# The down-projection's weight combinations of a hybrid decoder layer: summed by DMA in DRAM beside the input projection, instead of by VectorE during the up projection

## The chip, the cores and the metric

The kernel runs on one core of one Trainium2 chip. The metric is the device time of one execution in microseconds (us): the median of three runs before the change is 1322.26 us (1322.09 to 1323.52).

## The reference, cut to what matters

One layer of a decoder: an input projection into seven column groups, differential attention and a gated linear recurrence (HGRN2) on its parts, an output projection, and a feed-forward block with a short convolution. Sizes: 1024 tokens and 16 meta tokens, width 1024, feed-forward width 2816, all float32.

```python
a = rmsnorm(h, ln_mix_pre)
dq, dk, dv, hq, hf, hi, hg = split(a @ w_in)             # 28 column tiles of 128
mix = concat(diff_attention(dq, dk, dv), hgrn2(hq, hf, hi, hg)) @ w_out
h = h + rmsnorm(mix, ln_mix_post)
u = causal_conv3(rmsnorm(h, ln_ffn_pre) @ w_up) + conv_b # 2 x 2816 columns
gate, up = split(u)
y = (gelu(gate) * up) @ w_down                           # w_down is 2816 x 1024
h = h + rmsnorm(y, ln_ffn_post)
```

The change concerns `w_down`, cut into four quarters W11, W12, W21, W22 (1408 x 512 each).

## The kernel before, in words

**Precision.** Every float32 operand of a large product is split into a high part (a copy rounded to a shorter format, made by ScalarE) and a low part (raw minus high, made by GpSimd or VectorE: `split`, line 147). Three matmuls per pair of tiles (high x high, high x low, low x high) give the product.

**Stages, in order of time.** (1) Norm and transposes of the input, and the first three weight tiles. (2) The input projection: `dense` (line 726) takes 25 weight tiles, one after the other; each is loaded by two DMAs from SyncE (`load_m`, `load_split`, line 152), one tile ahead of its use, and split by ScalarE and GpSimd. A tile (hf, hq, hi, hg, dq, dk or dv of a head) is 3 groups of 24 matmuls. `interleave` (line 60) mixes these matmuls with attention (`attn`) or the recurrence (`hgrn_head`) of a head, whose products along a tree (`halve`, line 387: tiles `tt` and `t`) GpSimd makes too. (3) The output projection. (4) The up projection: 22 iterations `ft` (loop at line 1436; 0 and a part of 1 stand ahead of it), each with two token halves `p`. Products use a seven-multiplication scheme for 2 x 2 blocks (Strassen-Winograd), so sums of weight quarters and of partial results are formed: `unit` (line 1305) evacuates three banks, pa, pb and pc, through VectorE and ScalarE; the convolution's multiply-adds (tile `c`) are on VectorE too. (5) The down projection with the same scheme: 7 products x 11 steps.

**The part that changes.** Of the seven products of stage 5, four (numbers 5, 6, 7 and 4) need a combination of the quarters of `w_down`. These are formed ahead, during stage 4, by `down_sums` (line 1371): for each of 11 row blocks, four 128 x 512 tiles `wd` are loaded by SyncE, VectorE forms four differences, and SyncE stores each into a DRAM scratch `tsc`. One step of this generator is taken at four places of each iteration from `ft` 6 on (`SUMS`, line 35, and line 1442), so that its 55 steps last through `ft` 19. In stage 5 `w_in` (line 1396) loads the combinations back from `tsc` (tile `wi`).

**What orders the work.** TensorE's order is written out by hand. On the other engines a scheduler places instructions; `tc.issue_after(x)` holds an instruction back until `x` has been placed. Each engine takes its queue in order: an instruction that waits for a semaphore holds back all behind it. A DMA that SyncE or GpSimd issues can itself wait for an earlier DMA.

Of the kernel before, what the change touches and what calls it, by code (L numbers as in the profile page):

```python
# [9 lines left out]
F32 = mybir.dt.float32  # L10
# [3 lines left out]
ALU = mybir.AluOpType  # L14
# [17 lines left out]
WN = [258, 256]  # L32
C0 = [0, 514]
FA, FH, FO = 840, 800, 740
SUMS = 6


def start(i):
# [48 lines left out]
def layer_kernel(ctx: ExitStack, tc: tile.TileContext, x, meta, table, lbl, gpre, gpost, win,  # L87
# [59 lines left out]
    def split(hi, lo, raw, eng=None, after=None):  # L147
        A.copy(hi, raw)
        with nullcontext() if after is None else tc.issue_after(after.ins):
            (eng or G).tensor_tensor(lo, raw, hi.bitcast(F32), op=ALU.subtract)  # L150

    def load_split(src, name, where=None, bufs=4):
        raw = wp.tile([P, 512], F32, tag="wr", name=f"wr_{name}", bufs=3)
# [29 lines left out]
    last_load = []  # L183

    at_p_cm, ap_ = pool("attn", 1, "right")
    z_cm, zp = pool("pre", 2, "right")

    def load_m(m, name, where=None, bufs=4):
        return [load_split(win[m][:, 512 * c: 512 * (c + 1)], f"{name}_{c}", where, bufs) for c in range(2)]
# [533 lines left out]
                yield from values(i + 1)  # L723
        carry.append(pend.pop("tail"))

    def dense(tiles, preload=None):
        parts = preload
        for idx, (m, name, evac) in enumerate(tiles):
            if parts is None:
                parts = load_m(m, name)  # L730
            nxt = load_m(tiles[idx + 1][0], tiles[idx + 1][1]) if idx + 1 < len(tiles) else None
            for g in range(3):
                for step, c in enumerate(proj_group(g, parts, name, evac)):
                    if step == (8 if idx or g else 14):
                        flush()
                    yield c
            parts = nxt
# [190 lines left out]

    for h in range(HEADS):
        t_h, tiles_h = hgrn_in(h)  # L930
        interleave(dense(tiles_h), [attn(h, t_a)] + carried(), FA, 1500)
        if h < HEADS - 1:
            t_a, tiles_a = attn_in(h + 1)
            interleave(dense(tiles_a), [hgrn_head(t_h)] + carried(), FH, 1500)

    close(at_cm)
    wo_cm, wop = pool("wo", 7)
# [430 lines left out]
    for j in range(4, 7):  # L1368
        prep(7 + j)

    def down_sums():
        for k in range(NF // 2):
            b = {}
            for nm, kk, half in (("11", k, 0), ("12", k, 1), ("22", k + NF // 2, 1), ("21", k + NF // 2, 0)):
                b[nm] = dn.tile([P, 512], F32, tag="gk", name=f"wd{nm}_{k}")
                SY.dma_start(b[nm], wdown[P * kk: P * (kk + 1), 512 * half: 512 * (half + 1)])
            yield
            for j, d, p_, q_ in ((0, "11", "12", "11"), (2, "12", "22", "12"), (1, "22", "22", "11"), (3, "21", "21", "22")):
                V.tensor_tensor(b[d], b[p_], b[q_], op=ALU.subtract)
                SY.dma_start(tsc[j][P * k: P * (k + 1)], b[d])  # L1380
                yield

    NH = NF // 2
    LOOK = 3
    ORDER = (1, 2, 5, 6, 3, 7, 4)
# [19 lines left out]
    def operands(pr, k, loaded=None):  # L1405
        ga, gb, gc, gs = (keep[nm][:, k] if keep else None for nm in ("ga", "gb", "gc", "gs"))
        if pr == 1:
            a = loaded[0] if loaded else g_in(k, 0, "1")
        elif pr == 2:
            SY.dma_start(gb, g_src(k + NH, 0))  # L1410
            a = gb
        elif pr == 5:
            a = gs
        elif pr == 6:
            V.tensor_tensor(gs, gs, ga, op=ALU.subtract)
            a = gs
        elif pr == 3:
            V.tensor_tensor(gb, gb, gs, op=ALU.subtract)
            a = gb
        elif pr == 7:  # L1420
            V.tensor_tensor(ga, ga, gc, op=ALU.subtract)
# [12 lines left out]

    wd_sums = down_sums()
# [31 lines left out]
    def sums5(k):  # L1467
        SY.dma_start(keep["gc"][:, k], g_src(k, 1))
        b = g_in(k + NH, 1, "5")
        V.tensor_tensor(keep["gs"][:, k], keep["gc"][:, k], b, op=ALU.add)  # L1470
        SY.dma_start(keep["ga"][:, k], g_src(k, 0))

    steps = [(pr, k) for pr in ORDER for k in range(NH)]
# [36 lines left out]
    def evac(pr, m, py):  # L1510
        if pr == 1:
            A.copy(x1[:, m], py)
        elif pr == 2:
            V.tensor_tensor(c11[:, m], py, x1[:, m], op=ALU.add)
            squares(c11[:, m], m, 0)
            as_bias(m, 0)
            G.tensor_tensor(c11[:, m], c11[:, m], gfo[:, :512], op=ALU.mult)
        elif pr == 5:
            A.copy(x5[:, m], py)
        elif pr == 6:  # L1520
            V.tensor_tensor(u2[:, m], py, x1[:, m], op=ALU.add)
        elif pr == 3:
            c = u2[:, m]
            V.tensor_tensor(c, py, c, op=ALU.add)
            squares(c, m, 1)
            s_ = rstd(m, 1)
            hh = fp.tile([P, D], F32, tag="hh", name=f"hh{m}", bufs=2)
            SY.dma_start(hh, hsc[P * m: P * (m + 1), :])
            V.scalar_tensor_tensor(hh[:, :512], c11[:, m], s_, hh[:, :512], ALU.mult, ALU.add)
            G.tensor_tensor(c, c, gfo[:, 512:], op=ALU.mult)  # L1530
            V.scalar_tensor_tensor(hh[:, 512:], c, s_, hh[:, 512:], ALU.mult, ALU.add)
            SY.dma_start(out[P * m: P * (m + 1), :], hh)
        elif pr == 7:
            V.tensor_tensor(x1[:, m], py, x1[:, m], op=ALU.add)
            c = x5[:, m]
            V.tensor_tensor(c, c, x1[:, m], op=ALU.add)
            squares(c, 4 + m, 1)
            as_bias(4 + m, 1)
            G.tensor_tensor(c, c, gfo[:, 512:], op=ALU.mult)
        else:  # L1540
            c = x1[:, m]
            V.tensor_tensor(c, py, c, op=ALU.add)
# [99 lines left out]
```

## Time and profile before

| | |
|---|---|
| runs | 1322.26 us median |
| profiled execution | 1325.6 us, of which the span from first to last instruction is 1323.8 us |
| granted TensorE clock | 0.997 |
| busy: PE / DVE / ACT / POOL | 97% / 70% / 52% / 34% of the span |
| DMA | 165.00 MB, 123 GB/s of HBM traffic over the span |

PE is TensorE's matmuls, DVE is VectorE, ACT is ScalarE, POOL is GpSimd and SP is SyncE, which issues every DMA of the kernel before. In a row of a group or of a wait, `a<-b` means that tile a is written from tile b; L54 is the line of a helper that records every VectorE, ScalarE and GpSimd operation, so these are told apart by their tiles. "x11" counts instructions. A span time such as 820.69 counts from the first instruction.

### The profile page before, as it was taken

To read this page: it belongs to the slowest core of one execution; us is meant where nothing else is said; L and a number is where in the kernel's file an instruction comes from. 1 tells how busy PE (TensorE), PEld (TensorE's weight loads), DVE (VectorE), ACT (ScalarE), POOL (GpSimd) and SP (SyncE) were. 2 spreads that over 40 slices of the span, in tenths; PEclk is the share of its full clock that TensorE was granted. 3 is DMA by queue.
4 is the path that set the end of the run, shared out by engine and by line. 5 is a ranking of instruction groups with operands and counts; after the bars stand their busy time and mean duration, and the time that the engine had idled before them with its cause. 6 is when DMAs were issued, how large, how long until landed. Compare 5 with 4: busy or idle time off the path is not lost.

```text
span 1323.8 us, 26191 instructions
## 1 busy us (share of the span) xinstructions
PE 1286.8 (97%) x10172; PEld 1185.5 (90%) x10172; DVE 930.1 (70%) x1531; ACT 692.5 (52%) x1635; POOL 455.4 (34%) x340
## 2 busy tenths in 40 slices
PE   8999999999999999899999999999999999999997
PEld 7899999899999988677999999999999997888875
DVE  6464646465645564547997788989989967697586
ACT  8475466547544754246754444444444435454553
POOL 5211211121112111243077667676676730010121
PEclk9999999999999999999999999999999999999999
DMA  5111121112111335487232234545445428865363
GB/s 209 61 40 33 54 57 41 49 46 65 44 42 41 88 101 169 153 277 254 81 112 80 80 95 154 177 144 173 154 144 166 144 84 275 312 205 166 88 206 120
DMA packets 99427, 165.00 MB, mean 125 GB/s; under 512 B 10035, under 2 KB 34899, under 8 KB 99302
## 3 DMA queue, kind: packets, MB, share of 16 engines
q1 hardware_dynamic: 99302, 163.32, 37.8%
q8 instruction: 80, 1.31, 0.4%
q14 instruction: 45, 0.37, 0.1%
HBM read 122.65 MB, written 40.63 MB: 123 GB/s over the span
## 4 chain that ended last, share of the span: by engine, by line
PE 45%; DVE 11%; ACT 3%; issue 3%; DMA 2%; POOL 0%; SPq 0%; DVEq 0%; ACTq 0%; POOLq 0%
PE pd L1491 5%; PE pd L1492 5%; PE pd L1490 5%; DVE c L54 5%; PE pb L1316 4%; PE pb L1317 3%; PE pb L1318 3%; PE pa L1316 2%; PE pa L1317 2%; PE pa L1318 2%; PE pc L1316 2%; PE pc L1317 2%; PE pc L1318 2%; PE py L976 1%; PE py L972 1%
## 5 line engine op out<-in xcount | busy, mean ns | idle before, releaser
L1316 PE MATMUL pb<-t,uh 128*128 128x258 f32 x504 | 144.0, 286 | 8.9 <-DVE u L54 8.9
L1318 PE MATMUL pb<-t,ul 128*128 128x258 f32 x504 | 141.6, 281 | 0.0
L1317 PE MATMUL pb<-t,uh 128*128 128x258 f32 x504 | 141.6, 281 | 0.0
L1491 PE MATMUL pd<-wl,gh 128*128 128x512 f32 x308 | 122.0, 396 | 1.2 <-DVE wl L54 1.1
L1492 PE MATMUL pd<-wh,gl 128*128 128x512 f32 x308 | 121.7, 395 | 0.0
L1490 PE MATMUL pd<-wh,gh 128*128 128x512 f32 x308 | 121.7, 395 | 0.0
L54 POOL TENSOR_TENSOR c<-c,c 128x514 f32<-128x514 f32 (+1 forms) x44 | 75.2, 1709 | 121.1 <-ACT c L54 111.4
L1316 PEld LDWEIGHTS pb<-t,uh 128*128 128x128 f32 x504 | 95.4, 189 | 12.2 <-DVE u L54 12.1
L54 DVE SCALAR_TENSOR_TENSOR c<-uu,cwt,c 128x514 f32<-128x514 f32 (+1 forms) x88 | 89.2, 1023 | 19.3 <-ACT c L54 19.0
L1317 PEld LDWEIGHTS pb<-t,uh 128*128 128x128 f32 x504 | 95.6, 190 | 0.0
L1318 PEld LDWEIGHTS pb<-t,ul 128*128 128x128 f32 x504 | 95.2, 189 | 0.0
L1316 PE MATMUL pa<-t,uh 128*128 128x258 f32 (+1 forms) x336 | 95.2, 283 | 0.0
L1318 PE MATMUL pa<-t,ul 128*128 128x258 f32 (+1 forms) x336 | 95.0, 283 | 0.0
L1317 PE MATMUL pa<-t,uh 128*128 128x258 f32 (+1 forms) x336 | 94.8, 282 | 0.0
L1316 PE MATMUL pc<-t,uh 128*128 128x258 f32 (+1 forms) x336 | 94.4, 281 | 0.0
L1317 PE MATMUL pc<-t,uh 128*128 128x258 f32 (+1 forms) x336 | 94.0, 280 | 0.0
L1318 PE MATMUL pc<-t,ul 128*128 128x258 f32 (+1 forms) x336 | 93.7, 279 | 0.0
L54 DVE SCALAR_TENSOR_TENSOR c<-ug,cwt,c 128x514 f32<-128x514 f32 (+1 forms) x88 | 89.6, 1019 | 0.9 <-ACT c L54 0.6
L54 ACT CAST uh<-ra 128x512 fp32r<-128x512 f32 x67 | 41.0, 616 | 66.4 <-PE pb L1317 48.2
L1491 PEld LDWEIGHTS pd<-wl,gh 128*128 128x128 f32 x308 | 57.7, 187 | 16.5 <-DVE wl L54 2.7
L54 POOL TENSOR_TENSOR ul<-ws,uh 128x512 fp32r<-128x512 f32 x42 | 64.7, 1541 | 20.4 <-ACT uh L54 20.4
L1492 PEld LDWEIGHTS pd<-wh,gl 128*128 128x128 f32 x308 | 57.7, 187 | 14.4 <-DVE gl L54 0.4
(373 smaller groups left out, 4161.2 us busy)
## 6 DMA issues: line engine op xcount, KB each, us to landing
ra<-in_wup_dram SPq DMA_DIRECT2D x88, 256.0 KB, 3.0
mp<-msc SPq DMA_DIRECT2D x23, 512.0 KB, 6.0
wd<-in_wdown_dram SPq DMA_DIRECT2D x44, 256.0 KB, 3.3
tsc<-wd SPq DMA_DIRECT2D x44, 256.0 KB, 3.2
wi<-tsc SPq DMA_DIRECT2D x44, 256.0 KB, 2.9
gi<-gsc SPq DMA_DIRECT2D x33, 256.0 KB, 4.1
wi<-in_wdown_dram SPq DMA_DIRECT2D x33, 256.0 KB, 5.3
gsc<-c SPq DMA_DIRECT2D x22, 257.0 KB, 2.3
```

Source lines behind the costliest of these rows:

```text
L54: ins = call(*args, **kw)
L972: T.matmul(py[:r], mh, hi, start=(first and k == ks[0]), stop=False)
L976: T.matmul(py[:r], ml, hi, start=False, stop=(last and k == ks[-1]))
L1316: T.matmul(pt, hi[:, s], th[:, k], start=(first and k == 0), stop=False, skip_group_check=True)
L1317: T.matmul(pt, hi[:, s], tl[:, k], start=False, stop=False, skip_group_check=True)
L1318: T.matmul(pt, lo[:, s], th[:, k], start=False, stop=(k == 3), skip_group_check=True)
L1490: T.matmul(py, gh[:, s], wh, start=(k == 0 and pr not in (3, 7)), stop=False, skip_group_check=True)
L1491: T.matmul(py, gh[:, s], wl, start=False, stop=False, skip_group_check=True)
L1492: T.matmul(py, gl[:, s], wh, start=False, stop=(k == NH - 1), skip_group_check=True)
```

## The change

`down_sums` no longer uses VectorE or SBUF. Another choice of signs makes all four combinations sums (W12 + W11, W22 + W12, W22 + W12 + W11, and all four quarters), so that a DMA that adds into its destination can form them in DRAM. For each of the 11 row blocks SyncE issues four DRAM-to-DRAM copies of a quarter's block into `tsc`, and GpSimd issues four adding DMAs of 256 KB, cut into pieces of 512 bytes: two from `w_down`, then one from `tsc[0]` into `tsc[1]`, then one from `tsc[1]` into `tsc[3]`. A step ("tick") of the generator is taken per weight tile of the input projection; the stages of one row block are one tick apart, and a new row block begins every second tick, so that two tiles see four copies and four adds. The copies are held until the newest weight load on SyncE is placed, the adds until the newest low part made by GpSimd (`lows`) is placed. The 44 loads, 44 differences and 44 stores of the up projection are gone. The signs of the activations' sums and of the evacuations of stage 5 are turned to match; their number and kinds stay.

```diff
@@ split
-            (eng or G).tensor_tensor(lo, raw, hi.bitcast(F32), op=ALU.subtract)
+            low = (eng or G).tensor_tensor(lo, raw, hi.bitcast(F32), op=ALU.subtract)
+        if eng in (None, G):
+            lows.append(low)
...
+    def down_sums():
+        def quarter_of(k, r, c):
+            kk = k + NF // 2 * r
+            return wdown[P * kk: P * (kk + 1), 512 * c: 512 * (c + 1)]
+
+        def add(j, k, src):
+            with tc.issue_after(lows[-1].ins):
+                G.dma_start(tsc[j][P * k: P * (k + 1)], src, accum_op=ALU.add, max_dma_last_dim=512)
+
+        def copies(k):
+            for j, r, c in ((0, 0, 1), (2, 1, 1), (1, 1, 1), (3, 1, 0)):
+                with tc.issue_after(last_load[-1].ins):
+                    SY.dma_start(tsc[j][P * k: P * (k + 1)], quarter_of(k, r, c))
+
+        def firsts(k):
+            add(0, k, quarter_of(k, 0, 0))
+            add(2, k, quarter_of(k, 0, 1))
+
+        stages = ((0, copies), (1, firsts), (2, lambda k: add(1, k, tsc[0][P * k: P * (k + 1)])),
+                  (3, lambda k: add(3, k, tsc[1][P * k: P * (k + 1)])))
+        for tick in range(NF + 2):
+            for lag, do in stages:
+                k, rest = divmod(tick - lag, 2)
+                if rest == 0 and 0 <= k < NF // 2:
+                    do(k)
+            yield
+
+    wd_sums = down_sums()
...
-    def dense(tiles, preload=None):
+    def dense(tiles, preload=None, side=iter(())):
...
             nxt = load_m(tiles[idx + 1][0], tiles[idx + 1][1]) if idx + 1 < len(tiles) else None
+            next(side, None)
...
-    def down_sums():
-        for k in range(NF // 2):
-            b = {}
-            for nm, kk, half in (("11", k, 0), ("12", k, 1), ("22", k + NF // 2, 1), ("21", k + NF // 2, 0)):
-                b[nm] = dn.tile([P, 512], F32, tag="gk", name=f"wd{nm}_{k}")
-                SY.dma_start(b[nm], wdown[P * kk: P * (kk + 1), 512 * half: 512 * (half + 1)])
-            yield
-            for j, d, p_, q_ in ((0, "11", "12", "11"), (2, "12", "22", "12"), (1, "22", "22", "11"), (3, "21", "21", "22")):
-                V.tensor_tensor(b[d], b[p_], b[q_], op=ALU.subtract)
-                SY.dma_start(tsc[j][P * k: P * (k + 1)], b[d])
-                yield
...
-            if ft >= SUMS and j in (1, 3, 5, 6):
-                with tc.issue_after(marks["last"].ins):
-                    next(wd_sums, None)
```

TensorE's and ScalarE's orders are the same before and after. VectorE's queue before, at the turn from iteration 7 to iteration 8 of the up projection (`wd` are the weight quarters, `ul` low parts of up-weights, `u`, `x`, `ug` and `uu` the pieces of an iteration's evacuation, `c` the convolution):

```order
L54 TENSOR_TENSOR wd_1_9663<-wd_1_9665,wd_1_9663 128x512
L54 TENSOR_SCALAR c_7_1_9774<-ug_1_9542,cwt,c_7_1_9774 128x510
L54 TENSOR_TENSOR ul_9798<-ra_11_9787,uh_9797 128x512
L54 TENSOR_TENSOR ul_9842<-ws_9839,uh_9841 128x512
L54 TENSOR_TENSOR u_8_0_9804<-pb_0_9845,x_8_0_9803 128x258
L54 TENSOR_TENSOR u_8_1_9823<-pb_1_9859,x_8_1_9822 128x256
L54 TENSOR_TENSOR wd_1_9665<-wd_1_9665,wd_1_9661 128x512
L54 TENSOR_TENSOR ul_9908<-ws_9905,uh_9907 128x512
L54 TENSOR_TENSOR u_8_0_9805<-pb_0_9845,x_8_0_9803 128x258
L54 TENSOR_TENSOR uu_0_9802<-pc_0_9879,u_8_0_9805 128x258
```

and the same place now:

```order
L53 TENSOR_TENSOR ul_9858<-ra_11_9847,uh_9857 128x512
L53 TENSOR_SCALAR c_7_1_9836<-ug_1_9616,cwt,c_7_1_9836 128x510 x2
L53 TENSOR_TENSOR ul_9902<-ws_9899,uh_9901 128x512
L53 TENSOR_TENSOR u_8_0_9864<-pb_0_9905,x_8_0_9863 128x258
L53 TENSOR_TENSOR u_8_1_9883<-pb_1_9919,x_8_1_9882 128x256
L53 TENSOR_TENSOR ul_9966<-ws_9963,uh_9965 128x512
L53 TENSOR_TENSOR u_8_0_9865<-pb_0_9905,x_8_0_9863 128x258
L53 TENSOR_TENSOR uu_0_9862<-pc_0_9937,u_8_0_9865 128x258
```

The two `wd` differences are gone from between the evacuations; the rest keeps its sequence but for one low part that moves two rows up.

GpSimd's queue before, in the second head of the input projection, from the low part of tile dk to that of the next head's hf (`tt` and `t` are the recurrence's tree):

```order
L54 TENSOR_TENSOR wl_dk_1_3111<-wr_dk_1_3109,wh_dk_1_3110 128x512
L54 TENSOR_TENSOR tt_3130<-t_3131 128x130
L54 TENSOR_TENSOR wl_dv_0_3375<-wr_dv_0_3373,wh_dv_0_3374 128x512
L54 TENSOR_TENSOR tt_3130<-tt_3130 128x65
L54 TENSOR_TENSOR tt_3130<-tt_3130 128x32
L54 TENSOR_TENSOR tt_3130<-tt_3130 128x16
L54 TENSOR_TENSOR tt_3130<-tt_3130 128x8
L54 TENSOR_TENSOR wl_dv_1_3381<-wr_dv_1_3379,wh_dv_1_3380 128x512
L54 TENSOR_TENSOR wl_hf_0_3798<-wr_hf_0_3796,wh_hf_0_3797 128x512
```

and now:

```order
L53 TENSOR_TENSOR wl_dk_1_3154<-wr_dk_1_3152,wh_dk_1_3153 128x512
L53 DMA tsc<-in_wdown_dram 128x4x128 x2
L53 DMA tsc<-tsc 512x128
L53 TENSOR_TENSOR tt_3176<-t_3177 128x130
L53 TENSOR_TENSOR wl_dv_0_3421<-wr_dv_0_3419,wh_dv_0_3420 128x512
L53 TENSOR_TENSOR tt_3176<-tt_3176 128x65
L53 TENSOR_TENSOR tt_3176<-tt_3176 128x32
L53 TENSOR_TENSOR tt_3176<-tt_3176 128x16
L53 TENSOR_TENSOR tt_3176<-tt_3176 128x8
L53 TENSOR_TENSOR wl_dv_1_3427<-wr_dv_1_3425,wh_dv_1_3426 128x512
L53 DMA tsc<-tsc 512x128
L53 DMA tsc<-in_wdown_dram 128x4x128 x2
L53 DMA tsc<-tsc 512x128
L53 TENSOR_TENSOR wl_hf_0_3852<-wr_hf_0_3850,wh_hf_0_3851 128x512
```

Three adds stand ahead of the tree's product `tt<-t`, and four between wl_dv and wl_hf; of the four, the last one waits for the first one's completion. Blocks of four stand at six places of the projection.

SyncE's queue as the projection begins, before (`rb` and `rsc` are the attention's bias tables, on their way through DRAM):

```order
L156 DMA wr_hq_1_744<-in_win_dram 128x512
L308 DMA rsc<-rb_619 128x384
L156 DMA wr_hi_0_934<-in_win_dram 128x512
L308 DMA rsc<-rb_648 128x384
L156 DMA wr_hi_1_940<-in_win_dram 128x512
```

and now, where the first four copies stand among the tables' stores:

```order
L157 DMA wr_hq_1_744<-in_win_dram 128x512
L198 DMA tsc<-in_wdown_dram 128x512
L337 DMA rsc<-rb_619 128x384
L198 DMA tsc<-in_wdown_dram 128x512 x3
L157 DMA wr_hi_0_938<-in_win_dram 128x512
L337 DMA rsc<-rb_648 128x384
L157 DMA wr_hi_1_944<-in_win_dram 128x512
```

Before, the copy of a table out of PSUM by VectorE waited for the store of the previous table, which had the queue almost to itself; now one copy is ahead of the second table's store and three more are ahead of the third's.

More of the change, by code (lines that the diff above doesn't have):

```diff
@@ L34 @@
 FA, FH, FO = 840, 800, 740
-SUMS = 6
 def start(i):
@@ L181, in layer_kernel @@
     alo = atp.tile([P, KD, L], F32R, tag="alo", name="alo")
-    last_load = []
+    last_load, lows = [], []
+    def down_sums():
[21 more added lines that the diff above has]
+    wd_sums = down_sums()
     at_p_cm, ap_ = pool("attn", 1, "right")
@@ L930, in layer_kernel @@
         t_h, tiles_h = hgrn_in(h)
-        interleave(dense(tiles_h), [attn(h, t_a)] + carried(), FA, 1500)
+        interleave(dense(tiles_h, None, wd_sums), [attn(h, t_a)] + carried(), FA, 1500)
         if h < HEADS - 1:
             t_a, tiles_a = attn_in(h + 1)
-            interleave(dense(tiles_a), [hgrn_head(t_h)] + carried(), FH, 1500)
+            interleave(dense(tiles_a, None, wd_sums), [hgrn_head(t_h)] + carried(), FH, 1500)
     close(at_cm)
@@ L1414, in operands @@
         elif pr == 6:
-            V.tensor_tensor(gs, gs, ga, op=ALU.subtract)
+            V.tensor_tensor(gs, gs, ga, op=ALU.add)
             a = gs
         elif pr == 3:
-            V.tensor_tensor(gb, gb, gs, op=ALU.subtract)
+            V.tensor_tensor(gb, gs, gb, op=ALU.subtract)
             a = gb
         elif pr == 7:
-            V.tensor_tensor(ga, ga, gc, op=ALU.subtract)
+            V.tensor_tensor(ga, gc, ga, op=ALU.subtract)
             a = ga
@@ L1433, in operands @@
         return gh, gl, wh, wl
-    wd_sums = down_sums()
     for ft in range(1, NF):
@@ L1469, in sums5 @@
         b = g_in(k + NH, 1, "5")
-        V.tensor_tensor(keep["gs"][:, k], keep["gc"][:, k], b, op=ALU.add)
+        V.tensor_tensor(keep["gs"][:, k], b, keep["gc"][:, k], op=ALU.subtract)
         SY.dma_start(keep["ga"][:, k], g_src(k, 0))
@@ L1520, in evac @@
         elif pr == 6:
-            V.tensor_tensor(u2[:, m], py, x1[:, m], op=ALU.add)
+            V.tensor_tensor(u2[:, m], py, x1[:, m], op=ALU.subtract)
         elif pr == 3:
             c = u2[:, m]
-            V.tensor_tensor(c, py, c, op=ALU.add)
+            V.tensor_tensor(c, c, py, op=ALU.subtract)
             squares(c, m, 1)
@@ L1533, in evac @@
         elif pr == 7:
-            V.tensor_tensor(x1[:, m], py, x1[:, m], op=ALU.add)
+            V.tensor_tensor(x1[:, m], py, x1[:, m], op=ALU.subtract)
             c = x5[:, m]
-            V.tensor_tensor(c, c, x1[:, m], op=ALU.add)
+            V.tensor_tensor(c, x1[:, m], c, op=ALU.subtract)
             squares(c, 4 + m, 1)
@@ L1541, in evac @@
             c = x1[:, m]
-            V.tensor_tensor(c, py, c, op=ALU.add)
+            V.tensor_tensor(c, py, c, op=ALU.subtract)
             squares(c, 4 + m, 0)
```

## The prediction

> **What bounds the kernel now.** I read the page first, then TensorE's waits, then the stretches of the up projection. The page's busy times:
>
> ```profile
> PE 1286.8 (97%) x10172; PEld 1185.5 (90%) x10172; DVE 930.1 (70%) x1531; ACT 692.5 (52%) x1635; POOL 455.4 (34%) x340
> ```
>
> TensorE is the bound, and its own work isn't touched. Only the 37 us in which it idles, and time in which it restarts, can be won. TensorE's waits, summed by releaser, longest first:
>
> ```profile
> PE pb L1316 <- DVE u L54: 8.9, 13, 1.4
> PE pl L417 <- DVE hq L54: 3.7, 2, 2.6
> ```
>
> The largest is one place: bank pb of a new iteration of the up projection is free only when VectorE has made `u` out of it. Is that VectorE's load by the weight differences? The stretches tell it. Columns are us, then busy us and instructions of each engine, clock, DMA share, GB/s. The first stretch is the input projection beside which the adds will run; the second is iterations 3 to 6 of the up projection, the third 7 to 20:
>
> ```profile
> 63.00:470.00 407.00, 402.47 (x3927) 387.91 (x3926) 233.99 (x531) 235.03 (x691) 74.13 (x74) 1.00 0.18 52
> 707.60:787.30 79.70, 79.70 (x674) 79.70 (x673) 61.03 (x90) 38.37 (x68) 51.54 (x37) 1.00 0.25 81
> 787.30:1076.60 289.30, 282.88 (x2355) 280.12 (x2354) 256.79 (x352) 132.47 (x238) 199.15 (x124) 1.00 0.46 150
> ```
>
> An iteration is 168 matmuls. The second stretch has four iterations, 79.70 us, with no idle time at all and VectorE at 77%. The third has fourteen (2355 / 168), the same work plus the differences: VectorE at 89%, TensorE idle for 6.4 us. At the pace of the second stretch it would take 14 / 4 x 79.70 = 278.95 us; it takes 289.30. **The difference, 10.3 us, is what the differences cost**: 6.4 us of idle time and 3.9 us in slower restarts. How it comes about, in VectorE's timeline at the end of iteration 7:
>
> ```profile
> 817.98 1.10 DVE L54 TENSOR_TENSOR wd<-wd,wd 128x512 f32<-128x512 f32 x1
> 818.99 1.78 DVE L54 TENSOR_TENSOR ul<-ws,uh 128x512 fp32r<-128x512 f32 x1
> 820.69 0.41 DVE L54 TENSOR_TENSOR u<-pb,x 128x258 f32<-128x258 f32 x1
> ```
>
> `wd` pushes the low part `ul` back, `ul` the evacuations, and these the next iteration. VectorE is in arrears here, without a pause between rows.
>
> **The change part by part.**
>
> *The differences go.* The group of everything that touches `wd`, with durations as minimum, median and maximum in ns:
>
> ```profile
> L54 DVE TENSOR_TENSOR wd<-wd,wd x44: 676/1389/1578, 779.7 to 1055.0; 128x512 f32<-128x512 f32 x44
> L1380 SPq DMA_DIRECT2D tsc<-wd x44: 319/384/1922, 785.1 to 1056.5; - x44
> ```
>
> 44 x 1.39 = 61 us of VectorE's 257 in the third stretch go, four of them per iteration or 4.4 us; 79.70 us of the second stretch show what is left when they're absent. TensorE's order stays, so iterations 7 to 20 should take 19.93 us each: **-10.3 us**. What is late next? In iterations 3 to 6 nothing is, with the same casts, sums and convolution. The gain could be larger only through iterations 1 and 2, which have no differences; so 10.3 is also its upper end. Its lower end is 6.4, if the slow restarts have another cause. I take 10.3, since the second stretch holds the same instructions.
>
> The 44 loads and 44 stores on SyncE go as well. In that stage they free DMA share that no wait of TensorE names, so I count nothing. In the down projection the combinations are loaded as before, the signs turn and no instruction is added: nothing.
>
> *44 adds on GpSimd.* The profile has no DMA issued by GpSimd, so their price is bounded by other rows. Below: an issue on SyncE, 0.32 us (row above). Above: each of an add's 512 pieces is read and written, and GpSimd's own work on 512 columns takes 1.28 us, so twice that, 2.6 us. I take 1.3, the row on the same engine with the same count. Below nothing isn't possible, since the queue only gets longer. Where would it show? GpSimd is busy for 74 of 407 us in the first stretch; 44 adds would have to cost (407 - 74) / 44 = **7.6 us** each to fill it. Two places are tighter. GpSimd's queue around the second head's tile dk, then what VectorE needs from it, then TensorE's first use of the low part behind the block of four:
>
> ```profile
> 259.54 1.28 POOL L54 TENSOR_TENSOR wl_dk<-wr_dk,wh_dk 128x512 fp32r<-128x512 f32 x1 [0.80 <-ACT wh_dk L54]
> 272.19 0.40 POOL L54 TENSOR_TENSOR tt<-t 128x130 f32<-128x130 f32 x1 [11.36 <-DVE hq L54]
> ...
> 275.73 1.28 POOL L54 TENSOR_TENSOR wl_dv<-wr_dv,wh_dv 128x512 fp32r<-128x512 f32 x1
> 286.99 1.28 POOL L54 TENSOR_TENSOR wl_hf<-wr_hf,wh_hf 128x512 fp32r<-128x512 f32 x1 [9.98 <-ACT wh_hf L54]
> ```
>
> ```profile
> 277.15 0.70 DVE L54 TENSOR_TENSOR kr<-kr,tt 128x520 f32<-128x520 f32 x1
> ```
>
> ```profile
> 308.91 0.29 PE L207 MATMUL pi_hf<-ahi,wl_hf 128*128 128x272 f32 x1
> ```
>
> Three adds come between 260.82 and `tt<-t`, whose result VectorE reads at 277.15: each may cost (277.15 - 0.40 - 260.82) / 3 = **5.3 us** before anyone waits. Four come between 277.01 and wl_hf, which TensorE needs at 308.91: (308.91 - 1.28 - 277.01) / 4 = 7.7 us each. So 1.3 us, and 2.6 too, is covered by GpSimd's pauses: **0**. If that cover were gone, each us above 7.6 would cost up to 44 us.
>
> *The waits among them.* The last add of each block of four waits for the first one to land; behind it stand weight low parts. How long an add takes to land isn't shown either. The DMA issues with sizes and us to landing:
>
> ```profile
> wd<-in_wdown_dram SPq DMA_DIRECT2D x44, 256.0 KB, 3.3
> tsc<-wd SPq DMA_DIRECT2D x44, 256.0 KB, 3.2
> ...
> wr_hf<-in_win_dram SPq DMA_DIRECT2D x8, 256.0 KB, 2.8
> ```
>
> Between 3.2 us (one such store) and two loads and a store one after the other, 9.8 us. Even by the latter the block is through at 277.01 + 1.3 + 9.8 + 1.3 = 289.4 us, 2.4 us after wl_hf ran before, with TensorE's need at 308.91: **0**. The Trainium skill, in "DMA: Bandwidth & Descriptors" (Anatomy of one DMA), gives a DMA issued by GpSimd about 2.0 us plus its bytes at 436 GB/s, an estimate of 2.6 us for 256 KB; with it the sum is the same.
>
> *44 copies on SyncE, and traffic.* A weight tile's loads have a whole tile of lead, and a row's four copies stand behind them; a load of 2.8 us may double, at a DMA share of 0.18, without reaching the low parts' slack. Nothing, but for the beginning, where the copies stand among the bias tables' stores. SyncE's queue there and VectorE's:
>
> ```profile
> 49.02 0.32 SPq L308 DMA_DIRECT2D rsc<-rb  x1
> 51.19 0.33 SPq L156 DMA_DIRECT2D wr_hi<-in_win_dram  x1
> 53.02 0.32 SPq L308 DMA_DIRECT2D rsc<-rb  x1
> ```
>
> ```profile
> 57.89 0.38 DVE L54 TENSOR_REDUCE ident<-ident 128x32 f32<-128x128 f32 x1
> 61.93 0.19 DVE L54 TENSOR_TENSOR S<-S,rr 16x32 f32<-16x32 f32 x1 [3.65 <-PE S L614]
> ```
>
> The fourth table's copy waits for the third store, now behind three copies. If they drain one at a time that is 3 x 3.2 = 9.6 us, less VectorE's pause of 3.65: 6 us late at worst, and nothing if they overlap. I take 0.6 us, near nothing, because they are issued 2 us ahead of that store.
>
> *Sum.* Profiled execution 1325.6 - 10.3 + 0.6 = 1315.9 us. It lies 3.3 us above the median of the runs, 1322.26; from there **1312.6 us**. Its own range: 1310 (a larger gain is excluded; the runs spread by 1.4) to 1316 (only the 6.4 us).
>
> **The rivals.**
>
> *A. GpSimd's queue becomes the bound (slower).* Place: the low parts of the projection. It decides from 7.6 us per add; TensorE first lives on the lead of a low part, 308.91 - 288.27 = 20.6 us, so the break-even with the gain of 9.7 is at 7.6 + 30.3 / 44 = 8.3 us. At 9 us per add: 44 x 1.4 - 20.6 = 41 us lost, 1312.6 + 41 = 1354 us. For it: descriptors made in software, for 512 pieces, that no row prices. Against: six times the row I use.
>
> *B. Adds of 5.3 to 7.6 us.* Only the three ahead of `tt<-t` show: at 6.5 us, 3 x 1.2 = 3.6 us, which gives 1316. For it speaks what two engines do to each other here: `wd` takes 0.68 us alone and 1.39 in the median, beside GpSimd's products; 1.3 us so stretched is only 2.7.
> The Trainium skill, "SBUF — State Buffer" (A bandwidth-pool intuition that's wrong), speaks against this change: GpSimd cannot write descriptors while VectorE holds the shared port pair, and a DMA of 620 ns became 3100 ns. Five times my price would be 6.5 us, an estimate that lands in B; no run here shows it.
>
> *C. The gap stays, by another wait.* ScalarE's casts `uh` could end last once `wd` is gone, and half of the gain remain: 1317.5 us. Against: the four iterations without any idle time.
>
> *D. Contention in the projection eats the gain.* The adds move 256 KB from two sources each beside the loads, and GpSimd's queue beside VectorE's attention. TensorE idles only 4.5 of 407 us there; for no gain it would have to idle three times that, spread over four heads: 1322 us.
>
> **How the numbers follow.** Forecast 0.60 (1310 to 1316); B and C, 0.07 and 0.06 (1316 to 1319.6); D 0.08; A 0.19. A measurement of this kernel can tell about 0.2%, 2.6 us, from no change: faster is forecast, B and C, 0.73; same is D, 0.08; slower is A, 0.19. The range goes from 1309 to 1335: it holds all but A's larger part (above 8.5 us per add) and leaves out some 0.15.
>
> **What would show it.** Right: iterations 7 to 20 take 279 us with TensorE idle below 1 us, no row `pb <- DVE u` from there; the first stretch again has about 402 us busy in 407; GpSimd's DMA rows are below 2.6 us. Wrong: TensorE waiting for `wl` tiles, by GpSimd (A); for `pl` in the second head (B); for `u` behind `uh` (C); many short waits in the heads for `S`, `at` or `pb` (D); a new wait for `S` at 60 us (the copies).

## The result, and the profile after

The changed kernel takes **1314.15 us** (median of 6 runs, 1313.39 to 1315.30), the kernel before 1322.38 us beside it (1321.91 to 1323.52): a ratio of 0.9939, 95% interval 0.9929 to 0.9948. That is 8.2 us won, where 9.7 were forecast. The time lies in the range, and the kernel is faster by more than 0.2%; the forecast itself, 1312.6 us, or 0.9926 of the time before, is 1.5 us too low and just outside the interval.

The profiled execution of after takes 1313.97 us, span 1312.2. It is at the median of its runs, whereas that of before (1325.6) lay 3.3 us above its own. So the two profiles differ by 11.6 us and the medians by 8.2; where the surplus of 3.3 us lay is told with the third experiment.

The stretches of after come first: the input projection, beside which the adds now run, and iterations 7 to 20 of the up projection, in the columns of the table of before.

```profile
63.00:470.00 407.00, 401.56 (x3917) 386.86 (x3916) 233.94 (x530) 233.68 (x688) 123.81 (x118) 1.00 0.50 105
786.38:1065.45 279.07, 279.07 (x2355) 279.07 (x2353) 211.29 (x309) 134.66 (x238) 176.03 (x124) 1.00 0.22 76
```

The second row answers to the 289.30 us of before: the same 2355 matmuls, no idle time at all, VectorE at 76% in place of 89%. The first row has 407 us as before and TensorE busy in 401.56 of them, 0.9 us less than before; GpSimd is busy 49.7 us longer, or 1.13 us for each of the 44 adds; the share of the DMA engines rises from 0.18 to 0.50. TensorE's largest waits are now:

```profile
PE pl L446 <- DVE hq L53: 3.0, 2, 1.9
PE pb L1346 <- DVE u L53: 2.5, 2, 1.4
...
PE pl L455 <- issue: 1.0, 1, 1.0
```

The row on `u`, 8.9 us before, is down to the two waits of iterations 1 and 2. The last row is new. "issue" means that TensorE waited for nothing that the profile shows. The adds as a group, each row with the minimum, median and maximum of one instruction in ns on its queue, and what GpSimd idled for ahead of them:

```profile
L53 POOL DMA_DIRECT2D tsc<-in_wdown_dram x22: 1294/1750/2253, 78.4 to 437.9; - x22
L53 POOL DMA_DIRECT2D tsc<-tsc x22: 997/1045/2281, 95.2 to 469.9; - x22
...
  DMA tsc<-in_wdown_dram: 6.7, 3
  DMA tsc<-tsc: 3.2, 2
```

An add from `tsc` to `tsc` takes 1.0 us where no other add stands directly ahead (1.06 us at 95.2 us, with VectorE busy all the while), an add from `w_down` 1.3. The longer ones, up to 2.3 us, all stand behind another add, and their records overlap: such adds start 0.7 to 1.0 us apart. In the whole projection GpSimd idles 9.9 us for a landing, in five places. The issues with us to landing:

```profile
tsc<-in_wdown_dram SPq DMA_DIRECT2D x44, 256.0 KB, 4.9
...
tsc<-in_wdown_dram POOLq DMA_DIRECT2D x22, 256.0 KB, 7.2
tsc<-tsc POOLq DMA_DIRECT2D x22, 256.0 KB, 5.6
```

The tight place of the second head, in GpSimd's timeline:

```profile
259.61 1.28 POOL L53 TENSOR_TENSOR wl_dk<-wr_dk,wh_dk 128x512 fp32r<-128x512 f32 x1 [0.80 <-ACT wh_dk L53]
260.84 2.59 POOL L53 DMA_DIRECT2D tsc<-in_wdown_dram  x2
262.38 2.13 POOL L53 DMA_DIRECT2D tsc<-tsc  x1
272.27 0.40 POOL L53 TENSOR_TENSOR tt<-t 128x130 f32<-128x130 f32 x1 [7.76 <-DVE hq L53]
...
283.00 1.05 POOL L53 DMA_DIRECT2D tsc<-tsc  x1 [1.79 <-DMA tsc<-tsc]
288.30 1.27 POOL L53 TENSOR_TENSOR wl_hf<-wr_hf,wh_hf 128x512 fp32r<-128x512 f32 x1 [4.25 <-ACT wh_hf L53]
```

Behind three adds GpSimd still idles 7.76 us for VectorE before `tt<-t`, and behind the block of four 4.25 us before wl_hf. GpSimd delays nobody here. But TensorE, at the same moment:

```profile
272.71 0.74 PE L452 MATMUL pl<-hq,kr 128*32 128x16 f32 x64
274.46 0.21 PE L455 MATMUL pl<-hq,kr 128*16 128x8 f32 x2 [1.02 <-issue]
```

Sixty-four matmuls of 16 columns run in 0.74 us; then TensorE stands still for 1.02 us, and the profile shows nothing that it waits for. That is the new row, and several of the experiments are about it.

### The profile page after: what moved, and what is told of

Same layout as the page of the kernel before. It is cut to its first block, busy times and chain, and to the rows that moved or that the text cites. A ratio compares the mean times of both kernels' runs of the same rounds, so it can differ in the third digit from the quotient of the medians.

```text
span 1312.2 us, 26128 instructions
## 1 busy us (share of the span) xinstructions
PE 1283.2 (98%) x10172; PEld 1184.9 (90%) x10172; DVE 884.6 (67%) x1487; ACT 694.8 (53%) x1635; POOL 484.7 (37%) x384
## 3 DMA queue, kind: packets, MB, share of 16 engines
q8 instruction: 80, 1.31, 0.4%
## 4 chain that ended last, share of the span: by engine, by line
PE 83%; DVE 6%; ACT 4%; DMA 3%; issue 2%; POOL 2%; SPq 0%; DVEq 0%; ACTq 0%; POOLq 0%
PE pd L1505 5%; PE pd L1506 5%; PE pd L1504 5%; PE pb L1346 4%; PE pb L1347 4%; PE pb L1348 4%; PE pa L1346 3%; PE pa L1348 3%; PE pa L1347 3%; PE pc L1346 3%; PE pc L1347 3%; PE pc L1348 3%; PE pa L723 3%; PE pi_hf L232 1%; PE pi_dk L236 1%
## 5 line engine op out<-in xcount | busy, mean ns | idle before, releaser
L53 DVE SCALAR_TENSOR_TENSOR c<-uu,cwt,c 128x514 f32<-128x514 f32 (+1 forms) x88 | 97.2, 1105 | 19.6 <-ACT c L53 18.9
L53 POOL TENSOR_TENSOR c<-c,c 128x514 f32<-128x514 f32 (+1 forms) x44 | 63.6, 1445 | 122.7 <-ACT c L53 120.6
L1346 PE MATMUL pa<-t,uh 128*128 128x258 f32 (+1 forms) x336 | 95.2, 283 | 0.0
L1348 PEld LDWEIGHTS pb<-t,ul 128*128 128x128 f32 x504 | 95.2, 189 | 0.0
L53 POOL TENSOR_TENSOR ul<-ws,uh 128x512 fp32r<-128x512 f32 x42 | 60.7, 1444 | 35.4 <-ACT uh L53 35.4
L53 DVE TENSOR_TENSOR ul<-ra,uh 128x512 fp32r<-128x512 f32 x42 | 38.6, 920 | 48.1 <-ACT uh L53 48.1
```

The costliest lines, as they stand in the source:

```text
L53: ins = call(*args, **kw)
L1346: T.matmul(pt, hi[:, s], th[:, k], start=(first and k == 0), stop=False, skip_group_check=True)
L1348: T.matmul(pt, lo[:, s], th[:, k], start=False, stop=(k == 3), skip_group_check=True)
```

## The experiments

**What they were to tell apart.** The theory: the gap of 10.3 us is the differences on VectorE and nothing else, and the adds are hidden. First rival: the gap belongs to the transfers, or the surplus of the first profiled execution is part of it. Second rival: the adds cost TensorE something in the projection. Each experiment was timed in five rounds against the kernel before on the same chip.

**1 (e1). Before, without the 44 differences; loads and stores stay** (the stored quarters are then plain copies).

```diff
-                V.tensor_tensor(b[d], b[p_], b[q_], op=ALU.subtract)
                 SY.dma_start(tsc[j][P * k: P * (k + 1)], b[d])
```

> The kernel before, with the 44 differences on VectorE left out and its 44 loads and 44 stores kept (the stores write quarters instead of combinations, so four products use other weights). Theory (VectorE's arrears are the whole gap): iterations 7 to 20 take 279 us without idle time, and the time falls by the whole gain or more, to 1312 to 1315 us. Rival (SyncE's queue and DMA traffic of the up projection make the gap): iterations 7 to 20 stay near 289 us and the time stays within 2 us of the kernel before.

Measured: 1314.79 us (ratio 0.9949, 0.9937 to 0.9961). Its iterations 7 to 20:

```profile
791.06:1070.16 279.10, 279.10 (x2354) 279.10 (x2353) 211.87 (x309) 134.61 (x238) 175.84 (x124) 1.00 0.22 76
```

This is after's row, though the 88 transfers are still there. The rest of this run was not as expected: iterations 4 to 6 took 20.1, 22.1 and 23.6 us in its profiled execution, the slowest of its six (1318.82). Single operations of VectorE were longer there with no wait shown, for one a convolution step of 1.78 us at 748.5 that takes 0.75 in after in the median. Why they were longer stays open. The sixth iteration lost more than its wait: TensorE idled 1.84 us up to 778.0, and the granted clock was one half for the 3.41 us from 778.7 on.

**2 (e2). Before, with the differences, but only the first block's loads and stores** (the other differences work on the first block's data, and the down projection loads the first block's combinations throughout).

```diff
-                b[nm] = dn.tile([P, 512], F32, tag="gk", name=f"wd{nm}_{k}")
-                SY.dma_start(b[nm], wdown[P * kk: P * (kk + 1), 512 * half: 512 * (half + 1)])
+                if k == 0:
+                    b[nm] = dn.tile([P, 512], F32, tag="gk", name=f"wd{nm}_{k}")
+                    SY.dma_start(b[nm], wdown[P * kk: P * (kk + 1), 512 * half: 512 * (half + 1)])
...
-                SY.dma_start(tsc[j][P * k: P * (k + 1)], b[d])
+                if k == 0:
+                    SY.dma_start(tsc[j][P * k: P * (k + 1)], b[d])
```

> The kernel before, with the 44 differences kept on VectorE, but only the first row block's 4 loads and 4 stores (the differences run again and again on the same four tiles, and the down projection loads the first row block's combinations throughout). Theory: the differences alone hold VectorE up, so iterations 7 to 20 stay at 287 to 290 us and the time at 1320 to 1323 us. Rival (transfers): iterations 7 to 20 fall to about 279 us and the time to 1313 us.

Measured: 1321.45 us (0.9995, 0.9987 to 1.0004). Iterations 7 to 20 of this run, and then of the third, which is the kernel before once more:

```profile
785.12:1072.92 287.80, 282.79 (x2354) 280.04 (x2353) 257.86 (x352) 133.42 (x238) 198.38 (x124) 1.00 0.24 78
```

```profile
783.01:1072.46 289.45, 282.75 (x2355) 280.00 (x2353) 257.26 (x352) 132.00 (x238) 198.42 (x124) 1.00 0.45 150
```

With almost all of the transfers gone, the stretch is 1.65 us shorter; with the differences gone (first experiment), 10.3 us. Together the three rows settle the main term: the gap is VectorE's load.

**3 (e3). The kernel before, unchanged, once more.**

> The kernel before, unchanged, for a second profile and the spread of its runs. Iterations 7 to 20 take 289.3 us in the first profile, and that execution was 3.3 us above the median. If the gap of 10.3 us varies between executions, this profile shows another one, 8 to 9 us; if it does not, the 289 us come again and the missing 2 us of the gain lie elsewhere. Ratio 1.000.

Measured: 1321.68 us (0.9995, 0.9987 to 1.0004), its profiled execution 1321.48. The gap is the same, 289.45 - 279.07 = 10.4 us. This execution begins the up projection at 660.2 us and the first one of before began it at 664.5: the surplus of 3.3 us lay ahead of the up projection, most of it between the last head and there, in 3.2 us more from the fourth head's first `pi_hg` on (172.3 and 169.1 us). In that stretch of the first execution TensorE waited 2.57 us up to 544.7, and the granted clock was one half for the 3.41 us from 545.0 on, which is some 1.7 us of work; the second execution has no such place. The stretch takes 169.1 to 172.6 us in all the executions profiled here, with and without adds, so it tells nothing of the change.

**4 (e4, e6; e5). The changed kernel without its 44 adds, and the same again on the chip of the next runs.** The scratch quarters are then plain copies.

```diff
         def add(j, k, src):
-            with tc.issue_after(lows[-1].ins):
-                G.dma_start(tsc[j][P * k: P * (k + 1)], src, accum_op=ALU.add, max_dma_last_dim=512)
+            pass
```

> The changed kernel with the 44 copies on SyncE kept and the 44 adds on GpSimd left out (the four products use quarters instead of sums). Theory (the adds cost TensorE nothing in the end): the same time as the changed kernel within 1.5 us, 1313 to 1315 us; the pause of 1.2 us before a product pl at 274.5 us is gone, and a pause elsewhere returns. Rival (the adds eat 2 us of the gain): 1311 to 1312 us.

> The changed kernel without its 44 adds, once more (the four scratch quarters are then plain copies, so that the down projection multiplies by other weights; its amount of work is the same). Adds cost about 2 us: 1311 to 1312.5 us, below e5 by 1.5 to 3 us. The adds cost nothing and the difference was scatter: within 1 us of e5, both near 1313.

Measured: 1311.67 us (0.9924, 0.9911 to 0.9937), and 1313.30 us the second time (0.9931, 0.9918 to 0.9943). The first result looked like 2.5 us for the adds. The second one, beside the changed kernel once more on the same chip, brought it down:

> The changed kernel once more, beside the three runs that follow, so that they are compared on one chip. If the adds on GpSimd's queue cost TensorE some 2 us ahead of the up projection (the run without them, e4, came to 1311.67 us, the changed kernel to 1314.15): 1313 to 1315.5 us, some 2 us above e6, and no more of TensorE's stalls inside the up projection than before (iterations 3 to 20 at 19.93 us each). If the 2.5 us between those two were the scatter of executions: this run and e6 agree within 1 us, whichever is ahead.

Measured: 1314.45 us (0.9936, 0.9923 to 0.9949), so 1.15 us above its neighbour without adds, between the two expectations. The 12 runs of the changed kernel have a mean of 1314.07 us, the 10 without adds of 1312.60, each from two sets of runs: **1.5 us for the adds, give or take 1.3** (two standard errors, from spreads of 1.3 and 1.6). The medians say no more than that. The profiles say where at least a part of it lies, since one stretch of them hardly varies. It runs from the second head's first `pi_hg` (the product for its weight tile hg) to the third head's, in us:

| kernel | with 512-byte adds | from second to third `pi_hg` |
|---|---|---|
| before; before again; experiments 1 and 2 | no | 125.06; 125.07; 125.11; 125.10 |
| changed, without adds, twice | no | 125.10; 125.09 |
| changed; changed again | yes | 126.30; 126.35 |

The six profiled executions without adds agree within 0.05 us, copies or no copies; both with adds are 1.2 us longer. The pause at 274 us is in that stretch in both (1.02 and 1.05 us, "issue").

**What could TensorE wait for there?** It fetches its instructions by DMA: the profile's table of queues has a row for them, here for after between 260 and 275 us, and then for the second run without adds:

```profile
q1 hardware_dynamic: 1659, 1.96, 45.2%
q0 software_dynamic: 1584, 0.79, 44.8%
q8 instruction: 2, 0.03, 0.7%
```

```profile
q1 hardware_dynamic: 1666, 1.97, 41.8%
q8 instruction: 3, 0.05, 1.4%
```

The columns are packets, MB and the share of the engines' time. The adds' queue (q0) puts 1584 packets beside the 1659 of the copies and weight loads, and one of the three fetches has left the window. The fetch records tell when: in four executions without adds (before twice, the copies twice) the one of this place stands at 269.0 to 269.7 us, in the two of the changed kernel at 272.1 and 272.6. A fetch is 16 KB (1.31 MB in 80, in the whole run). Among the wide matmuls they come 15 to 19 us apart and around the small ones 5 to 6 (in before at 229.0, 248.4, 263.1, 269.0 and 274.1 us): 64 small ones are through in 0.74 us. That they are TensorE's shows in the count: between two of them it begins 256 matmuls and weight loads in the median, in before and in after. So the theory became: **the adds' packets delay a fetch of TensorE's instructions, and it shows where the matmuls are small.**

**5 (e9). The changed kernel without the three adds ahead of `tt<-t` in the second head.**

```diff
-                if rest == 0 and 0 <= k < NF // 2:
+                if rest == 0 and 0 <= k < NF // 2 and tick != 11:
```

> The changed kernel without the three adds that stand ahead of tt<-t in the second head (two tsc<-in_wdown_dram and one tsc<-tsc from 260.84 us on; three quarter tiles then keep their plain copies, all else is as in the changed kernel). Theory: their packets hold up one fetch of TensorE's instructions. In the four runs without adds in which it was looked up, the fetch of that place stands at 269.0 to 269.7 us, in the changed kernel's two profiles at 272.1 and 272.6, and TensorE then waits 1.0 and 1.1 us ('issue') at pl<-hq,kr at 274.5. If so: the fetch is back at 269 to 270 us, no 'issue' row stands at 274 us, and the stretch from the first pi_hg of the second head to that of the third is 125.1 us, as in all six runs without adds, and not 126.3. The median falls by about 1 us, which these rounds hardly tell. Rival: the pause comes from the copies or from a place in TensorE's program that any shift of its instructions brings about: then it stays, and the stretch is 126.3.

Measured: the fetch is back at 269.7 us, the stretch takes 125.20 us. TensorE at the place of the pause:

```profile
272.70 0.71 PE L452 MATMUL pl<-hq,kr 128*32 128x16 f32 x62
273.24 0.17 PE L455 MATMUL pl<-hq,kr 128*16 128x8 f32 x1
273.24 0.20 PE L452 MATMUL pl<-hq,kr 128*32 128x16 f32 x2
273.26 0.17 PE L455 MATMUL pl<-hq,kr 128*16 128x8 f32 x1
273.37 0.44 PE L234 MATMUL pi_dq<-alo,wh_dq 128*128 128x384 f32 x1
```

No pause: the theory held, and the rival that the copies or the mere shift of the program cause it fell. The median, 1313.70 us (0.9924, 0.9911 to 0.9938), can't show 1 us. The profiled execution was the slowest of its runs (1317.84), and it shows the same thing at the next head's small matmuls, with TensorE's pace right behind it in the columns of the stretches:

```profile
394.31 0.62 PE L452 MATMUL pl<-hq,kr 128*32 128x16 f32 x50
397.24 0.28 PE L452 MATMUL pl<-hq,kr 128*32 128x16 f32 x12 [2.32 <-issue]
```

```profile
397.90:401.31 3.41, 3.41 (x13) 3.41 (x12) 1.54 (x4) 0.62 (x1) 1.16 (x2) 0.50 0.02 5
```

Its fetch there stands at 394.8 us (393.3 in after, 390.5 to 391.4 without adds). Behind the pause the granted clock is one half for 3.41 us, some 1.7 us of work. So the price isn't one fixed pause: it depends on how the fetches fall among the adds, and a long pause costs more than its length.

**6 (e10, e11). Every step of the dealing one weight tile later; and the same with pieces of 2048 bytes.** One `yield` ahead of the loop over the ticks does it; the second run has `max_dma_last_dim=2048` as well.

> The changed kernel with every step of the dealing one weight tile later (same 44 copies and 44 adds). If the pause hangs on which adds lie ahead of the small matmuls pl<-hq,kr: the three-add block moves away from 261 us, a block of one or two of the other kind takes its place, the pause at 274 us goes or moves to the same matmuls of another head (first and third at about 148 and 400 us), and the median is within 1 us of the changed kernel's, 1313 to 1315 us. If each add costs GpSimd's own work something instead: no row of POOL shows it now, and the time is the same too, but the pause at 274 us stays.

> One tile later and in pieces of 2048 bytes, the version meant to lose least of the gain: 1.1 and 0.8 us per add on GpSimd, and neither block of three ahead of the second head's small matmuls. If pauses of TensorE's fetch are the adds' whole price: 0 to 1 us over the kernel without adds (1312.6 us, mean of its ten runs): 1312.5 to 1313.5 us, at most 1 us below the changed kernel, which the interval hardly tells. If longer waits among the adds with large pieces (7.8 us before three adds at 2048 bytes, 5.3 before two at 512) come ahead of a difference that is waited for: 1314 us or more.

Measured: 1316.15 us (0.9949, 0.9935 to 0.9963) and 1315.66 us (0.9941, 0.9929 to 0.9953). In both the stretch of the second head is 125.2 us, and in both the pause has moved to 395 us, the same matmuls of the third head, with 1.7 and 1.0 us:

```profile
PE pl L453 <- issue: 1.7, 1, 1.7
```

That the pause moves with the adds was expected; the times were not. The first run lies above its 1313 to 1315 us. The second was to take 1312.5 to 1313.5, or 1314 and more by the expectation's other branch, and 1315.66 fits only that one; whether for the reason given there, longer waits among the adds, no profile of it shows. Neither version beats the changed kernel measurably.

**7 (e7, e8). Pieces of 2048 and of 256 bytes in place of 512**, the same bytes in 128 and 1024 pieces per add.

> The adds in pieces of 2048 bytes in place of 512: a quarter as many pieces, the same bytes. If the adds' price goes by the number of pieces (what GpSimd writes for each, and the packets that stand ahead of other queues' packets), one add falls from 1.0 to 1.3 us on GpSimd to 0.4 to 0.6 us, TensorE's loss of about 2 us falls to 0.5 to 1 us, and the time is 1311.5 to 1313 us, below both kernels. If the price goes by the bytes: GpSimd's time for one add may fall, the landing times stay at 5.6 to 7.2 us and the time stays at 1313 to 1315.5 us. Third possibility: larger pieces spread over fewer transfer engines or hold each of them longer, the landing grows to 10 us or more, the waits among the adds (2.8 us at most now) grow with it, and the time is 1315 us or more.

> The adds in pieces of 256 bytes: twice as many pieces, the same bytes. The forecast's rival A said that GpSimd's queue becomes the bound from 7.6 to 8.3 us per add. If the price goes by pieces and nothing else: 2.0 to 2.6 us per add on GpSimd, which the fills of 5.3 to 7.7 us per add still hold, TensorE's loss grows from about 2 to about 4 us, 1315 to 1317.5 us. If twice the pieces make an add's landing twice as long (11 to 14 us) and GpSimd cannot write the next add until the one before has landed, an add costs GpSimd 8 us or more in the blocks of four, the casts' differences (the lows) come late there, TensorE waits for them, and the time is 1325 us or more, slower than before the change. If the price goes by bytes: 1313 to 1315.5 us.

Measured with 2048: 1313.69 us (0.9940, 0.9926 to 0.9954), the same as with 512. The add gets cheaper on GpSimd, less than expected; its rows with 2048, then with 256:

```profile
L53 POOL DMA_DIRECT2D tsc<-tsc x22: 802/822/1447, 95.3 to 469.9; - x22
```

```profile
L53 POOL DMA_DIRECT2D tsc<-tsc x22: 1282/1318/1335, 95.1 to 475.9; - x22
```

Medians of 0.82, 1.05 and 1.32 us for 128, 512 and 1024 pieces, of the adds within `tsc`, lie on a line: 0.75 us and 0.57 ns for each piece. The landing doesn't follow the pieces (medians 6.7 and 5.7 us with 2048, 7.2 and 5.6 with 512). In the second head the larger pieces cost TensorE less: the fetch stands at 271.4 us, the stretch takes 125.48, 0.4 us more than without adds. In the third head this run has a pause of 0.5 us at 395.9, and the median shows no gain.

Measured with 256: **1321.05 us** (0.9986, 0.9974 to 0.9998), 6.6 us above the changed kernel on the same chip. The whole gain but 0.14% is gone, though an add's own time grew by 0.3 us. GpSimd's waits show why:

```profile
POOL tsc L53 <- issue: 92.8, 20, 9.1
```

GpSimd stands for 92.8 us before 20 of the 44 adds, up to 9.1 us, and for nothing that the profile shows (another 36.8 us before ten more are put down to VectorE and TensorE, from which an add takes nothing). The expectation's condition fits it, that the next add can't be written until an earlier one has landed: with 512-byte pieces such a row has 2.0 us. What it waits for isn't shown, and none of the three forecasts (1313 to 1315.5, 1315 to 1317.5, 1325 and more) came. How TensorE loses by it is seen at 366 us, in GpSimd's, VectorE's and TensorE's rows:

```profile
366.11 1.32 POOL L53 DMA_DIRECT2D tsc<-tsc  x1 [5.32 <-PE pt L699]
366.90 3.04 POOL L53 TENSOR_TENSOR wl_dq<-wr_dq,wh_dq 128x512 fp32r<-128x512 f32 x2
```

```profile
366.87 3.12 DVE L53 TENSOR_TENSOR ast<-ast 128x1 f32<-128x1 f32 x1
```

```profile
371.54 0.79 PE L723 MATMUL pa<-avn,az 128*128 128x128 f32 x2 [3.25 <-ACT pb L53]
```

The adds held GpSimd back, so two products that make weight low parts stand in a row behind them (in after they run 4.75 us apart). VectorE's `ast`, one element per partition and 0.16 us in the median, runs beside them and takes 3.12 us; ScalarE's `pb` needs it, and TensorE idles 3.25 us. Between 63 and 500 us five operations of VectorE take 2.0 to 3.1 us, four of them beside two such products in a row and one beside another product; with 512-byte pieces none is above 1.3. The third head, from its first `pi_hg` to the fourth's, takes 132.5 us here and 125.8 in after. Of these 6.7 us, 3.25 are that wait, some 1.7 the half clock that the record shows for 3.41 us from 371.5 on, and 0.9 a late fetch at 400.7. The clock is lower in all twelve runs together: 0.9953 on average, against 0.9977 in the twelve of the changed kernel, which by itself would be 3.2 of 1321 us. The Trainium skill, in "SBUF — State Buffer" (A bandwidth-pool intuition that's wrong), tells of the other direction, GpSimd kept from writing descriptors by VectorE's use of a port; this run shows VectorE kept waiting by GpSimd's products, and no run shows an add with 512-byte pieces that took five times its 1.0 us (2.3 us at most).

**All thirteen profiles together.** Where no add or one stands on GpSimd between 260 and 268 us, the fetch of that place begins at 268.8 to 270.0 us (ten profiles); where three stand there, at 271.4 (pieces of 2048 bytes), 272.1 and 272.6. And of all the pauses of 0.3 us or more that the profiles mark "issue" on TensorE, fifteen, each ends 2.2 to 2.5 us after a fetch began, which ties the pause to the fetch. But not every one belongs to the adds. At the fourth head's small matmuls, 532 to 536 us and so behind the last add at 470, five executions have such a pause, two of them of kernels without adds (0.43 us in the second experiment, 1.84 in the first run of the copies alone, which has one of 0.42 at 142 us too). So a fetch can be late without any add; what held it up there isn't shown.

## Why the prediction was nearly right

**The differences go, -10.3 us: right.** Iterations 7 to 20 went from 289.30 to 279.07 us, with nothing late next: no row on `u` or `uh` behind iteration 2, so rival C didn't come. Experiments 1 and 2 show the cause of the whole gap: the slower restarts belong to it too (the lower bound of 6.4 us would have left them out).

**The price of an add on GpSimd, 1.3 us: right** (1.0 to 1.3 where none stands directly ahead, 1.13 on the average of the busy time), though it was the row of another operation with the same count, so the closeness is in part luck. The covering of the queue was right as well: `tt<-t` and wl_hf weren't late. Rival B didn't show.

**The waits among the adds, 0: right.** The bounds of 3.2 and 9.8 us hold the medians of 5.6 and 7.2; the block of four was through at 284.05 us, before 289.4. The estimate of 2.6 us from the Trainium skill, "DMA: Bandwidth & Descriptors" (Anatomy of one DMA), was less than half of the 5.6 and 7.2 us that the trace gives for adds between two places in DRAM; the sum didn't hang on it.

**The copies at the start, +0.6 us: too much.** The delay came, but VectorE's pause covered it: the third table's copy waited 1.47 us for a store (`rsc<-rb`) and ran at 53.37 us, 51.98 before; the fourth's at 57.27, 56.00 before; yet `S<-S,rr` ran at 62.00 us, 61.93 before. Before the change no such copy waited for a store by the profile: its rows name TensorE's `pb`.

**The step that failed is "traffic: nothing", and with it the 0 of the adds.** The prediction looked for what the adds could delay among the weight loads, and rightly found slack (a load of wr_hf went from 2.8 to 5.2 us, and no wait on it was added). It didn't ask who else is served by the DMA engines. TensorE's own instructions are, and a fetch some 3 us late behind the adds' packets costs 1.0 to 1.2 us at the small matmuls of the second head: shown by experiment 5 for that place, argued for the others. By the means the adds cost 1.5 us, give or take 1.3. With -10.3 and +1.5 on 1322.4 us one gets 1313.6; the 0.5 us that remain to the 1314.15 are within what runs differ by. Rival D named contention in the projection, but as many short waits for `S`, `at` or `pb`, and at a price for no gain; it came as a small part of that and by another way.

**Taking off the surplus of the profiled execution, 3.3 us: right.** It belonged to the stretch ahead of the up projection and not to what was removed, as the third experiment shows.

**Rival A didn't come, but its threshold was wrong.** It was to decide from 7.6 us per add, an average fill of GpSimd's time. With 256-byte pieces an add costs 1.4 us and 92.8 / 44 = 2.1 us of waiting, 3.5 in all (4.4 with the other 36.8 us), and 6.6 us are lost. What decides isn't the average: single waits last up to 9.1 us, and at the place followed above the work that they push together keeps VectorE, and so TensorE, waiting. The half clock behind such waits, for which the prediction's rival has no term, makes up about half of the 6.6 us by the average clock above.

## What to carry to other kernels

Price a removed load by comparing stretches of the same loop with and without it: that gave 10.3 us here, and the measured stretch came out at 10.2. When work is moved to DMA beside a saturated TensorE, slack in every named wait doesn't make it free; look also at where many tiny matmuls use up instructions, and at transfers that no line of the kernel issues. A queue's average fill says little when single waits are long: look at the longest one, and at what runs back to back after it. And look at the granted clock right behind a long pause before you price the pause.

## What the runs showed of the hardware

TensorE's instruction fetches stand in the table of DMA queues beside the kernel's transfers (80 fetches, 1.31 MB, one for 256 matmuls and weight loads in the median), and one came 2.4 to 3.6 us later with the adds' packets about (269.0 to 269.7 us without, 272.1 and 272.6 with); at 64 matmuls in 0.74 us that stopped TensorE for 1 us. All fifteen such pauses in the thirteen profiles end 2.2 to 2.5 us after a fetch began, also the three of them in kernels without adds.

Eight times in these profiles, the first and last microseconds aside, the granted clock falls to one half, always for 3.41 us, and it begins within 1.5 us of the end of an idle time of TensorE: 1.57, 1.82, 1.84 (twice), 1.85, 2.32, 2.57 and 3.25 us long. One of 1.91 us wasn't followed by it, nor was any other below 1.8.

An accumulating DMA of 256 KB within the scratch in DRAM costs GpSimd 0.75 us and 0.57 ns per piece (128 to 1024 pieces); with 512 pieces it lands after 5.6 us in the median, one from `w_down` after 7.2. With 1024 pieces GpSimd waits up to 9.1 us ahead of an add, with 512 there is one such wait, of 2.0.

Two products of 128x512 on GpSimd back to back (3.04 us) ran beside a VectorE operation on one element per partition, which took just that long: 3.12 us in place of 0.16.
